# Weight splits, the norm's sum and the order of seven products moved in a two-layer RG-LRU and attention trunk

## The chip, the cores and the metric

The kernel runs on one core of a Trainium2 chip. The metric is the time of one execution on the device in microseconds, as the median of several runs. Three runs of the kernel before took 1909.01, 1909.31 and 1905.85 us, with a median of 1909.01. The profile is of one further execution.

## The reference

The model has two layers on 512 tokens of width 1024, all in float32. Each layer adds half a gated FFN, a mixer, and half a second gated FFN. The mixer is a gated linear recurrence in layer 0 and stick-breaking attention in layer 1; keys and values are projected once, between the layers.

```python
def rms_norm(x, gain):
    xf = x.astype(jnp.float32)
    y = xf * lax.rsqrt(jnp.mean(xf * xf, axis=-1, keepdims=True) + EPS)
    return (y * gain.astype(jnp.float32)).astype(x.dtype)

def swiglu(h, w13, w2):
    gate, up = jnp.split(h @ w13, 2, axis=-1)
    return (jax.nn.silu(gate) * up) @ w2

# per layer: x += 1/2 swiglu(rms_norm(x)); x += mixer(rms_norm(x)); x += 1/2 swiglu(rms_norm(x))
```

The hidden width of an FFN is 2816. The change touches the four FFNs and what prepares them.

## The kernel before

**Layout and precision.** The residual x lies in SBUF as eight tiles of 128 channels by 512 tokens. Each float32 operand is split into a high part in the rounded format that TensorE takes (a cast) and a low part (the operand minus its high part). A product of two operands is three matmuls: high by high, high by low, low by high. A full product of a weight tile of 128 outputs by 1024 inputs with x is so 3 x 8 = 24 matmuls of 128 x 512 (`product`).

**Weights.** The class `Weights` holds a list of all weight tiles in the order of use. SyncE's queue loads a tile into a buffer w_raw, ScalarE casts it to w_hi (L85, in some places GpSimd, L87), and VectorE or GpSimd subtracts to get w_lo (L89); the last argument of `plan_w` names the engine of the low part. Tiles are prepared four ahead of the one in use. There are five buffers each of w_hi and w_lo and seven of w_raw.

**The FFN.** Its 22 tiles of hidden channels are worked off in three groups (8, 8 and 6), each followed by eight down products. The first tiles of an FFN are plain ones (six in ffn1 of layer 0, four in ffn2 of both layers, none in ffn1 of layer 1): a gate product pg and an up product pu take x times the gain without the norm's factor, and `swish` multiplies both by the factor r afterwards. All further tiles come in pairs, whose four blocks of weights by two halves of tokens are computed with seven products of half size in place of eight, 24 matmuls of 128 x 256 each, in the order of the table `FORMS`. An entry names a block of weights (a11, a12, a21, a22 as loaded; s1 to s4 are sums that VectorE forms at L114), one of three PSUM banks X, Y, Z that it is added to, and which of the seven forms of the operands it takes. After some of the products a copy on ScalarE or an add or subtraction on VectorE takes what the bank holds (L386 to L397). There are 37 such pairs: 8, 9, 11 and 9.

**Operands of the pairs.** `normed` makes them for two of the eight tiles of x at a time, so it is called four times per FFN: x times gain times r on VectorE, four sums, and the casts and low parts of seven forms (hh and hl). It needs r.

**The norm.** `Norm.add` squares a tile of x on ScalarE and adds it on VectorE to acc; `rstd` sums acc over the channels with one matmul, ss, and turns it into r (three activations on ScalarE, three operations on VectorE, the last gives rs). In the first FFN the squares come with the splits of x at the start, in `split_x`; there pg and pu of tile 0 are issued interleaved, and rstd stands after tile 1. In the two ffn2 the products pg and pu of tile 0 are interleaved by `product2` (seven eighths of both, then the rest), and rstd follows them. Behind rstd, `normed` is called twice and then `swish` of the oldest plain tile, until no tile waits.

**Order.** A scheduler orders the instructions of all engines; at the start the orders of VectorE, SyncE and ScalarE are those of the code (`manual_schedule`). Each engine works its list in order. PSUM has eight banks, given out in turn to the products.

Of the kernel before, what the change touches and what calls it, by code (L numbers as in the profile page):

```python
# [7 lines left out]
F32 = mybir.dt.float32  # L8
# [4 lines left out]
P = 128  # L13
S = 512
D = 1024
KT = D // P
# [6 lines left out]
BLOCKS = ("a11", "a21", "a22", "a12")  # L23
SUMS = {"s3": ("a11", "a21"), "s1": ("a21", "a22"), "s2": ("s1", "a11"), "s4": ("s2", "a12"), **{b: None for b in BLOCKS}}

FORMS = (("a11", "X", 4), ("s3", "Y", 0), ("s2", "X", 1), ("a12", "Z", 5), ("s1", "X", 2), ("a22", "Y", 3), ("s4", "X", 6))
HS = S // 2
NH = 16
HD = 64
# [120 lines left out]
def trunk(ctx, tc, a, out):  # L150
# [60 lines left out]
    def plan_w(key, src, hi="act", lo="dve", cols=1024):  # L211
        plan.append((key, src, cols, hi, lo))

    def plan_ffn(n, l):
        nf = PLAIN[n, l]
        for lo, hi in THIRDS:
            for i in range(lo, hi):
                if i < nf:

                    for j, g in enumerate("gu"):  # L220
                        plan_w((n, l, g, i), a[f"{n}_w13"][l, j, i], lo="pool" if i > 0 else "dve")
                elif i % 2 == 0:
                    for f in FORMS:
                        plan_w((n, l, i, f[0]), a[f"{n}_s13"][l, i // 2])
            for m in range(KT):
                plan_w((n, l, "d", lo, m), a[f"{n}_w2"][l, m, :, lo * P:hi * P], cols=(hi - lo) * P)
# [22 lines left out]
    W = Weights(nc, plan, wp)  # L249
# [102 lines left out]
    def ffn(n, l, ht, g, rs, after, full=False, hn=None):  # L352
# [2 lines left out]
        hn = [] if hn is None else hn  # L355

        def swish(i, pg, pu, act):
            e = cur.ep.tile([P, 4, S], F32, tag="e", name=f"e{n}{l}{i}")
            tg, tu = e[:, 0], e[:, 1]
            nc.vector.tensor_tensor(out=tg, in0=pg, in1=r, op=ALU.mult)  # L360
            last_silu.append(nc.scalar.activation(out=tg, in_=tg, func=AF.Silu))
            nc.vector.tensor_tensor(out=tu, in0=pu, in1=r, op=ALU.mult)
            nc.vector.tensor_tensor(out=tu, in0=tu, in1=tg, op=ALU.mult)
            act.append(split(tu, "a", f"a{n}{l}{i}"))

        def pair(i, act):
# [3 lines left out]
            for f, (name, bank, form) in enumerate(FORMS):  # L370
                hi, lo = W.get((n, l, i, name))
                new = bank not in banks
                if new:
                    banks[bank] = psum(f"p{bank}{n}{l}{i}")
                ps = banks[bank]
                for c in range(2):
                    o = ps[:, c * HS:(c + 1) * HS]
                    for j in range(KT // 2):
                        ws = slice(c * S + j * P, c * S + j * P + P)
                        xh, xl = hn[j][0][:, form], hn[j][1][:, form]  # L380

                        mm(o, hi[:, ws], xh, new and c == 0 and j == 0, False)
                        mm(o, hi[:, ws], xl, False, False)
                        mm(o, lo[:, ws], xh, False, j == KT // 2 - 1)

                if f == 0:  # L386
                    nc.scalar.copy(out=e[:, 0], in_=ps)  # L387
                elif f == 1:
                    nc.scalar.copy(out=e[:, 2], in_=ps)
                elif f == 2:  # L390
                    nc.scalar.copy(out=e[:, 1], in_=ps)
                elif f == 3:
                    nc.vector.tensor_tensor(out=e[:, 0], in0=ps, in1=e[:, 0], op=ALU.add)
                elif f == 4:
                    nc.vector.tensor_tensor(out=e[:, 2], in0=ps, in1=e[:, 2], op=ALU.subtract)
                elif f == 5:
                    nc.vector.tensor_tensor(out=e[:, 1], in0=ps, in1=e[:, 1], op=ALU.subtract)  # L397
# [13 lines left out]
        for lo_t, hi_t in THIRDS:  # L411
            act = []
            for i in range(lo_t, hi_t):
# [3 lines left out]
                    continue  # L417
                pg, pu = psum(f"pg{n}{l}{i}"), psum(f"pu{n}{l}{i}")
                wg = W.get((n, l, "g", i))
                if i == lo_t:  # L420
                    product2(pg, wg, pu, W.get((n, l, "u", i)), ht, full and lo_t == 0)
                else:
                    product(pg, wg, ht)
                    product(pu, W.get((n, l, "u", i)), ht)
                queue.append((i, pg, pu, act))
                if r is None:
                    if full and i == 0:
                        continue
                    r = rs()
                while queue:  # L430
                    for _ in range(2):
                        if len(hn) < KT // 2:
                            hn.append(normed(len(hn), g, r, f"{n}{l}"))
                    swish(*queue.pop(0))
# [30 lines left out]
    def split_x(k0, k1):  # L465
        for m in range(k0, k1):
            h.append(split_gain(x[m], gain(G_FFN1[0], m), "a", f"h0_{m}"))
            n0.add(m, x[m], [])

    phase_ffn()  # L470
    with tc.manual_schedule(engines={mybir.EngineType.DVE, mybir.EngineType.SP, mybir.EngineType.Activation}):
        W.first(2, ((0, 1), (1, 2), (2, 4), (4, 6), (6, 8)), load_x, split_x)
    late = {}

    def start():
# [224 lines left out]
    for p in range(NPAIR):  # L700
# [19 lines left out]
        run(gen)  # L720
        run(pend)
        pend = gen
        if p in (3, 5, 7):
            h3.append(normed(len(h3), G_FFN1[1], r3, "n3"))

    def v_out(g, pv):
        vt = dp.tile([2, 4, P, NCH, P], F32, tag="vd", name=f"vd{g}", bufs=2)
# [9 lines left out]
    for g in range(2):  # L737
# [5 lines left out]
        for c in range(4):  # L743
# [8 lines left out]
                    mm(pv[s], xl[:, ss], hi[:, ks], False, c == 3 and k == 1)  # L752
            if g == 0 and c < 2:
                run(pend)
            if g == 0 and c == 2:
                h3.append(normed(len(h3), G_FFN1[1], r3, "n3"))
            if g == 1 and c == 0:
                v_out(0, pvs[0])
# [305 lines left out]
```

## Time and profile before

| what | value |
|---|---|
| median of three runs | 1909.01 us |
| profiled execution | 1906.09 us |
| its span, first to last instruction | 1904.4 us |
| TensorE busy | 1846.8 us, 97% |
| VectorE busy | 1392.7 us, 73% |
| ScalarE busy | 921.5 us, 48% |
| GpSimd busy | 216.3 us, 11% |
| HBM traffic | 108 GB/s over the span |

The profile is read from the whole to the part: the busy shares say which engine could set the end, the table of stretches says where that engine was not busy, the list of its waits says for what, and a timeline shows what the engine that it waited for was doing. A group of rows gives a mean over all places where a line runs, so a single wait is found in the timeline alone.

### The profile page before, as it was taken

What the parts mean: (1) busy time and instruction counts of PE and PEld (TensorE: products, weight loads), DVE (VectorE), ACT (ScalarE), POOL (GpSimd) and SP (SyncE); (2) the same over time, 40 slices, a digit from 0 to 9 for tenths busy, and PEclk for the clock granted to TensorE, in tenths of its full rate; (3) what the DMA queues carried; (4) which work ended last, traced back from release to release, by engine and by line L of the source; (5) the groups of instructions that cost most, each with busy time, mean ns of one, the idle gap of its engine ahead of it and who ended that gap; (6) DMA issues with size and microseconds to landing.
All of it is one profiled execution on the core that took longest, in us unless ns stands there. A gap on an engine that the chain in (4) does not pass through costs nothing. (4 is left out here: it accounts for less than half of the span.)

```text
span 1904.4 us, 27318 instructions
## 1 busy us (share of the span) xinstructions
PE 1846.8 (97%) x11040; PEld 1635.3 (86%) x11040; DVE 1392.7 (73%) x1687; ACT 921.5 (48%) x1282; POOL 216.3 (11%) x218
## 2 busy tenths in 40 slices
PE   8899999999999999999899999999888999999999
PEld 6789989887788899897689999898676788999897
DVE  6876757688869577476978658575899869667573
ACT  4434525476645245255545435244578745445251
POOL 5100000021220000000200000000366530000000
PEclk9999999999999999999999999999999999999999
DMA  6132513222423234132363424234365431424131
GB/s 222 56 90 88 150 57 115 67 79 89 144 78 103 86 102 142 45 111 77 122 218 115 133 78 125 86 96 141 125 190 144 146 103 54 133 78 145 66 106 61
DMA packets 73118, 207.87 MB, mean 109 GB/s; under 512 B 7584, under 2 KB 17056, under 8 KB 72480
## 3 DMA queue, kind: packets, MB, share of 16 engines
q1 hardware_dynamic: 72704, 205.81, 35.4%
q8 instruction: 86, 1.41, 0.3%
q10 hardware_dynamic: 288, 0.32, 0.1%
q14 instruction: 40, 0.33, 0.1%
HBM read 189.85 MB, written 16.25 MB: 108 GB/s over the span
## 5 line engine op out<-in xcount | busy, mean ns | idle before, releaser
L85 ACT CAST w_hi<-w_raw 128x1024 fp32r<-128x1024 f32 (+1 forms) x165 | 165.5, 1007 | 287.0 <-PE pdffn L201 82.5
L85 ACT CAST w_hi<-w_s 128x1024 fp32r<-128x1024 f32 x148 | 155.3, 1049 | 238.1 <-PE pdffn L201 104.7
L201 PE MATMUL pXffn<-hhffn,w_hi 128*128 128x256 f32 x832 | 236.7, 285 | 4.7 <-ACT hhffn L342 2.0
L201 PE MATMUL pXffn<-hlffn,w_hi 128*128 128x256 f32 x832 | 236.3, 284 | 0.9 <-DVE hlffn L343 0.8
L201 PE MATMUL pXffn<-hhffn,w_lo 128*128 128x256 f32 x832 | 235.9, 284 | 0.0
L89 DVE TENSOR_TENSOR w_lo<-w_raw,w_hi 128x1024 fp32r<-128x1024 f32 (+3 forms) x169 | 193.1, 1145 | 54.6 <-ACT w_hi L85 49.1
L201 PE MATMUL pdffn<-ahffn,w_hi 128*128 128x512 f32 x592 | 230.8, 390 | 0.3
L201 PE MATMUL pdffn<-alffn,w_hi 128*128 128x512 f32 x592 | 230.7, 390 | 0.0
L201 PE MATMUL pdffn<-ahffn,w_lo 128*128 128x512 f32 x592 | 230.4, 389 | 0.0
L89 DVE TENSOR_TENSOR w_lo<-w_s,w_hi 128x1024 fp32r<-128x1024 f32 x148 | 180.9, 1222 | 45.1 <-ACT w_hi L85 44.8
L85 ACT CAST w_hi<-w_a 128x1024 fp32r<-128x1024 f32 x111 | 116.5, 1049 | 171.0 <-PE pdffn L201 70.7
L201 PEld LDWEIGHTS pXffn<-hhffn,w_hi 128*128 128x128 f32 x832 | 160.1, 192 | 6.5 <-ACT effn L387 2.3
L89 DVE TENSOR_TENSOR w_lo<-w_a,w_hi 128x1024 fp32r<-128x1024 f32 x111 | 135.6, 1222 | 35.8 <-ACT w_hi L85 35.8
L201 PEld LDWEIGHTS pXffn<-hlffn,w_hi 128*128 128x128 f32 x832 | 160.3, 193 | 1.7 <-DVE hlffn L343 1.3
L201 PEld LDWEIGHTS pXffn<-hhffn,w_lo 128*128 128x128 f32 x832 | 160.3, 193 | 0.0
L440 DVE SCALAR_TENSOR_TENSOR x<-pdffn,x 128x512 f32<-128x512 f32 x72 | 49.8, 691 | 137.1 <-PE pdffn L201 137.1
L201 PEld LDWEIGHTS pdffn<-ahffn,w_hi 128*128 128x128 f32 x592 | 111.2, 188 | 24.6 <-ACT ahffn L407 1.8
L201 PEld LDWEIGHTS pdffn<-alffn,w_hi 128*128 128x128 f32 x592 | 111.2, 188 | 24.3 <-DVE alffn L408 1.0
L201 PEld LDWEIGHTS pdffn<-ahffn,w_lo 128*128 128x128 f32 x592 | 111.1, 188 | 22.6
L201 PE MATMUL pYffn<-hlffn,w_hi 128*128 128x256 f32 x416 | 117.9, 283 | 0.2 <-DVE hlffn L347 0.2
L201 PE MATMUL pYffn<-hhffn,w_hi 128*128 128x256 f32 x416 | 117.8, 283 | 0.0
L201 PE MATMUL pYffn<-hhffn,w_lo 128*128 128x256 f32 x416 | 117.7, 283 | 0.0
(1150 smaller groups left out, 4786.5 us busy)
## 6 DMA issues: line engine op xcount, KB each, us to landing
w_a<-in_ffn_s SPq DMA_DIRECT2D x148, 512.0 KB, 3.7
w_raw<-in_ffn_w SPq DMA_DIRECT2D x90, 512.0 KB, 3.8
w_raw<-in_ffn_w SPq DMA_DIRECT2D x32, 384.0 KB, 3.2
w_raw<-in_w_in SPq DMA_DIRECT2D x16, 512.0 KB, 3.6
qp<-qd SPq DMA_DIRECT2D x14, 512.0 KB, 5.3
w_raw<-in_w_out SPq DMA_DIRECT2D x8, 512.0 KB, 3.7
w_raw<-in_w_k SPq DMA_DIRECT2D x8, 512.0 KB, 3.6
w_raw<-in_w_v SPq DMA_DIRECT2D x8, 512.0 KB, 3.7
```

Of the source, the lines that this page charges most:

```text
L85: nc.scalar.copy(out=hi[:, cs], in_=raw[:, cs])
L89: eng.tensor_tensor(out=lo[:, cs], in0=raw[:, cs], in1=hi[:, cs].bitcast(F32), op=ALU.subtract)
L201: nc.tensor.matmul(o, l, r, start=start, stop=stop, skip_group_check=True)
L440: nc.vector.scalar_tensor_tensor(out=x[m], in0=pd, scalar=0.5, in1=x[m], op0=ALU.mult, op1=ALU.add)
```

## The change

The six edits are: the low parts of the plain tiles' weights are made on VectorE, where GpSimd made those of all plain tiles but the first of each FFN; the squares and adds of the first norm come after all splits of the start; in the first FFN `swish` comes ahead of two `normed`, and tiles 0 and 1 of every FFN take other buffers for it; in the two ffn2, pg of tile 0 is a product by itself, rstd follows it, then pu; the operands of the second layer's first FFN are made among the products of the values instead of those of the keys; and the seven products have another order.

```diff
--- before.py
+++ after.py
@@ -23,7 +23,7 @@
 BLOCKS = ("a11", "a21", "a22", "a12")
 SUMS = {"s3": ("a11", "a21"), "s1": ("a21", "a22"), "s2": ("s1", "a11"), "s4": ("s2", "a12"), **{b: None for b in BLOCKS}}
 
-FORMS = (("a11", "X", 4), ("s3", "Y", 0), ("s2", "X", 1), ("a12", "Z", 5), ("s1", "X", 2), ("a22", "Y", 3), ("s4", "X", 6))
+FORMS = (("a11", "X", 4), ("a12", "Z", 5), ("s2", "X", 1), ("s3", "Y", 0), ("s1", "X", 2), ("a22", "Y", 3), ("s4", "X", 6))
 HS = S // 2
 NH = 16
 HD = 64
@@ -216,9 +216,8 @@
         for lo, hi in THIRDS:
             for i in range(lo, hi):
                 if i < nf:
-
                     for j, g in enumerate("gu"):
-                        plan_w((n, l, g, i), a[f"{n}_w13"][l, j, i], lo="pool" if i > 0 else "dve")
+                        plan_w((n, l, g, i), a[f"{n}_w13"][l, j, i])
                 elif i % 2 == 0:
                     for f in FORMS:
                         plan_w((n, l, i, f[0]), a[f"{n}_s13"][l, i // 2])
@@ -355,8 +354,11 @@
         hn = [] if hn is None else hn
 
         def swish(i, pg, pu, act):
-            e = cur.ep.tile([P, 4, S], F32, tag="e", name=f"e{n}{l}{i}")
-            tg, tu = e[:, 0], e[:, 1]
+            if i < 2:
+                tg, tu = temp("sq", f"tg{n}{l}{i}"), temp("acc", f"tu{n}{l}{i}")
+            else:
+                e = cur.ep.tile([P, 4, S], F32, tag="e", name=f"e{n}{l}{i}")
+                tg, tu = e[:, 0], e[:, 1]
             nc.vector.tensor_tensor(out=tg, in0=pg, in1=r, op=ALU.mult)
             last_silu.append(nc.scalar.activation(out=tg, in_=tg, func=AF.Silu))
             nc.vector.tensor_tensor(out=tu, in0=pu, in1=r, op=ALU.mult)
@@ -385,11 +387,11 @@
 
                 if f == 0:
                     nc.scalar.copy(out=e[:, 0], in_=ps)
-                elif f == 1:
+                elif f == 3:
                     nc.scalar.copy(out=e[:, 2], in_=ps)
                 elif f == 2:
                     nc.scalar.copy(out=e[:, 1], in_=ps)
-                elif f == 3:
+                elif f == 1:
                     nc.vector.tensor_tensor(out=e[:, 0], in0=ps, in1=e[:, 0], op=ALU.add)
                 elif f == 4:
                     nc.vector.tensor_tensor(out=e[:, 2], in0=ps, in1=e[:, 2], op=ALU.subtract)
@@ -417,7 +419,12 @@
                     continue
                 pg, pu = psum(f"pg{n}{l}{i}"), psum(f"pu{n}{l}{i}")
                 wg = W.get((n, l, "g", i))
-                if i == lo_t:
+                if i == 0 and not full:
+
+                    product(pg, wg, ht)
+                    r = rs()
+                    product(pu, W.get((n, l, "u", i)), ht)
+                elif i == lo_t:
                     product2(pg, wg, pu, W.get((n, l, "u", i)), ht, full and lo_t == 0)
                 else:
                     product(pg, wg, ht)
@@ -427,6 +434,12 @@
                     if full and i == 0:
                         continue
                     r = rs()
+                if full:
+                    while queue:
+                        swish(*queue.pop(0))
+                        for _ in range(2):
+                            if len(hn) < KT // 2:
+                                hn.append(normed(len(hn), g, r, f"{n}{l}"))
                 while queue:
                     for _ in range(2):
                         if len(hn) < KT // 2:
@@ -465,11 +478,12 @@
     def split_x(k0, k1):
         for m in range(k0, k1):
             h.append(split_gain(x[m], gain(G_FFN1[0], m), "a", f"h0_{m}"))
-            n0.add(m, x[m], [])
 
     phase_ffn()
     with tc.manual_schedule(engines={mybir.EngineType.DVE, mybir.EngineType.SP, mybir.EngineType.Activation}):
         W.first(2, ((0, 1), (1, 2), (2, 4), (4, 6), (6, 8)), load_x, split_x)
+        for m in range(KT):
+            n0.add(m, x[m], [])
     late = {}
 
     def start():
@@ -720,8 +734,6 @@
         run(gen)
         run(pend)
         pend = gen
-        if p in (3, 5, 7):
-            h3.append(normed(len(h3), G_FFN1[1], r3, "n3"))
 
     def v_out(g, pv):
         vt = dp.tile([2, 4, P, NCH, P], F32, tag="vd", name=f"vd{g}", bufs=2)
@@ -752,7 +764,7 @@
                     mm(pv[s], xl[:, ss], hi[:, ks], False, c == 3 and k == 1)
             if g == 0 and c < 2:
                 run(pend)
-            if g == 0 and c == 2:
+            if g == 0 and c > 0 or g == 1 and c == 1:
                 h3.append(normed(len(h3), G_FFN1[1], r3, "n3"))
             if g == 1 and c == 0:
                 v_out(0, pvs[0])
```

**VectorE at the start.** h0_5l to h0_7l are the low parts of the last tiles of x, acc_n0 is the running sum of squares (sq_n00 to sq_n07), w_lo0 and w_lo1 the low parts of tile 0's two weights, w_lo2 and up those of the tiles after it. Before:

```order
L318 SCALAR_TENSOR_TENSOR h0_5l_180<-x1_79,prm_75,h0_5h_179 128x512
L292 TENSOR_TENSOR acc_n0_137<-acc_n0_137,sq_n05_183 128x512
L89 TENSOR_TENSOR w_lo0_107<-w_raw0_105,w_hi0_106 128x256
L89 TENSOR_TENSOR w_lo1_110<-w_raw1_108,w_hi1_109 128x256
L318 SCALAR_TENSOR_TENSOR h0_6l_191<-x1_79,prm_75,h0_6h_190 128x512
L292 TENSOR_TENSOR acc_n0_137<-acc_n0_137,sq_n06_194 128x512
L318 SCALAR_TENSOR_TENSOR h0_7l_198<-x1_79,prm_75,h0_7h_197 128x512
L292 TENSOR_TENSOR acc_n0_137<-acc_n0_137,sq_n07_201 128x512
L486 TENSOR_SCALAR ident_952<-cf_948 128x128
```

And now:

```order
L317 SCALAR_TENSOR_TENSOR h0_5l_164<-x1_79,prm_75,h0_5h_163 128x512
L89 TENSOR_TENSOR w_lo0_107<-w_raw0_105,w_hi0_106 128x256
L89 TENSOR_TENSOR w_lo1_110<-w_raw1_108,w_hi1_109 128x256
L317 SCALAR_TENSOR_TENSOR h0_6l_172<-x1_79,prm_75,h0_6h_171 128x512
L317 SCALAR_TENSOR_TENSOR h0_7l_176<-x1_79,prm_75,h0_7h_175 128x512
L289 COPY acc_n0_181<-sq_n00_179 128x512
L89 TENSOR_TENSOR w_lo2_209<-w_raw2_207,w_hi2_208 128x1024
L291 TENSOR_TENSOR acc_n0_181<-acc_n0_181,sq_n01_183 128x512
L89 TENSOR_TENSOR w_lo3_215<-w_raw3_213,w_hi3_214 128x1024
L291 TENSOR_TENSOR acc_n0_181<-acc_n0_181,sq_n02_186 128x512
L89 TENSOR_TENSOR w_lo4_221<-w_raw4_219,w_hi4_220 128x1024
```

The seven adds that stood between the splits, and the one after them, now stand behind the last split, with a low part of a weight between each two.

**VectorE behind the first norm's factor.** rs_n0 is r; pgffn100 and puffn100 are the products of tile 0, effn100 and effn101 what `normed` works on (before, effn100_382 is the buffer of swish of tile 0). Before, the last of the rows between the factor (row 44 of VectorE) and the end of the first swish:

```order
L343 TENSOR_TENSOR hlffn101_371<-effn101_367,hhffn101_370 128x512
L345 TENSOR_TENSOR effn101_367<-effn101_367 128x256
L347 TENSOR_TENSOR hlffn100_356<-effn100_352,hhffn100_355 128x1024
L345 TENSOR_TENSOR effn101_367<-effn101_367 128x256 x3
L349 SCALAR_TENSOR_TENSOR hlffn101_371<-effn101_367,hhffn101_370 128x256
L360 TENSOR_TENSOR effn100_382<-pgffn100_205,rs_n0_343 128x512
L362 TENSOR_TENSOR effn100_382<-puffn100_206,rs_n0_343 128x512
L347 TENSOR_TENSOR hlffn101_371<-effn101_367,hhffn101_370 128x1024
L114 TENSOR_TENSOR w_s3_13_610<-w_a11_12_574,w_a21_12_576 128x1024
L363 TENSOR_TENSOR effn100_382<-effn100_382 128x512
```

And now, from the factor on:

```order
L308 SCALAR_TENSOR_TENSOR rt_n0_344<-ss_n0_341,rt_n0_344 128x512
L309 SCALAR_TENSOR_TENSOR rs_n0_343<-rt_n0_344,rs_n0_343 128x512
L310 TENSOR_SCALAR rs_n0_343<-rs_n0_343 128x512
L362 TENSOR_TENSOR tgffn100_352<-pgffn100_205,rs_n0_343 128x512
L364 TENSOR_TENSOR tuffn100_353<-puffn100_206,rs_n0_343 128x512
L335 SCALAR_TENSOR_TENSOR effn100_362<-x0_78,prm_75,rs_n0_343 128x512 x2
L344 TENSOR_TENSOR effn100_362<-effn100_362 128x256
L365 TENSOR_TENSOR tuffn100_353<-tuffn100_353,tgffn100_352 128x512
L344 TENSOR_TENSOR effn100_362<-effn100_362 128x256
L335 SCALAR_TENSOR_TENSOR effn101_377<-x0_78,prm_75,rs_n0_343 128x512
L342 TENSOR_TENSOR hlffn100_366<-effn100_362,hhffn100_365 128x512
```

The reads of tile 0's two products now follow the factor at once; before, thirteen rows on operands (45 to 57) stood between. The swish of tile 1 moved with it: it was 38 rows behind the factor and is 19 rows behind it now.

**ScalarE in a pair.** effn216 is the buffer of a pair in the last FFN, pXffn216 and pYffn216 its banks; w_hi369 and up are casts of weights. Before, around the three copies:

```order
L85 CAST w_hi367_15073<-w_s1_365_14999 128x1024
L85 CAST w_hi368_15103<-w_a22_363_14934 128x1024
L387 COPY effn216_15072<-pXffn216_15077 128x512
L407 CAST ahffn214_15064<-effn214_14838 128x512
L407 CAST ahffn215_15068<-effn214_14838 128x512
L85 CAST w_hi369_15135<-w_s4_369_15133 128x1024
L389 COPY effn216_15072<-pYffn216_15107 128x512
L85 CAST w_hi370_15165<-w_raw370_15164 128x1024
L391 COPY effn216_15072<-pXffn216_15077 128x512
```

And now:

```order
L85 CAST w_hi367_15079<-w_s1_365_15003 128x1024
L85 CAST w_hi368_15109<-w_a22_363_14940 128x1024
L409 CAST ahffn214_15070<-effn214_14844 128x512
L409 CAST ahffn215_15074<-effn214_14844 128x512
L389 COPY effn216_15078<-pXffn216_15083 128x512
L85 CAST w_hi369_15141<-w_s4_369_15139 128x1024
L393 COPY effn216_15078<-pXffn216_15083 128x512
L85 CAST w_hi370_15171<-w_raw370_15170 128x1024
L391 COPY effn216_15078<-pYffn216_15176 128x512
L85 CAST w_hi371_15203<-w_raw371_15202 128x1024
```

The copy of the bank Y stood second of three and now stands last, with one cast between it and the copy of X ahead of it.

## Rows read from the trace of the kernel before

**Rows 1.** The page, busy us, share of the span and instructions by engine.

```profile
PE 1846.8 (97%) x11040; PEld 1635.3 (86%) x11040; DVE 1392.7 (73%) x1687; ACT 921.5 (48%) x1282; POOL 216.3 (11%) x218
```

**Rows 2.** Table of stretches: busy us (instructions) by engine, TensorE's clock, DMA share, GB/s.

```profile
0.00:50.00 50.00, 43.70 (x168) 33.76 (x169) 35.29 (x54) 24.33 (x34) 27.14 (x26) 0.93 0.63 211
50.00:100.00 50.00, 43.21 (x216) 36.59 (x214) 43.82 (x61) 23.71 (x32) 6.93 (x2) 0.93 0.20 56
550.00:600.00 50.00, 46.17 (x241) 39.91 (x240) 45.18 (x66) 27.51 (x38) 5.85 (x3) 0.97 0.21 64
1600.00:1650.00 50.00, 47.68 (x349) 45.24 (x350) 41.24 (x48) 25.94 (x35) 0.00 (x0) 1.00 0.48 148
```

**Rows 3.** Waits of TensorE: what waited, for whom, us in total, times, longest.

```profile
PE hsk L201 <- POOL thk L661: 8.2, 6, 2.6
PE pgffn L201 <- DVE effn L360: 5.4, 1, 5.4
PE pXffn L201 <- ACT hhffn L342: 2.0, 1, 2.0
PE pZffn L201 <- DVE w_lo L89: 2.0, 1, 2.0
PE pgffn L201 <- DVE h_7l L318: 1.9, 1, 1.9
PE pXffn L201 <- ACT effn L387: 1.7, 2, 1.5
PE pgffn L201 <- DVE h_6l L318: 1.4, 1, 1.4
PE pXffn L201 <- ACT w_hi L85: 1.0, 1, 1.0
PE pgffn L201 <- DVE h_2l L318: 0.9, 1, 0.9
PE pXffn L201 <- DVE hlffn L343: 0.8, 1, 0.8
PE pgffn L201 <- DVE h_4l L318: 0.8, 1, 0.8
```

**Rows 4.** Table of stretches again: behind three waits, and three others to compare.

```profile
23.50:29.50 6.00, 5.94 (x14) 4.68 (x15) 5.45 (x5) 2.09 (x2) 5.17 (x4) 0.50 0.68 209
30.00:45.00 15.00, 15.00 (x66) 12.02 (x65) 6.05 (x12) 4.80 (x6) 6.62 (x4) 1.00 0.47 140
45.00:75.00 30.00, 26.59 (x118) 21.69 (x116) 30.00 (x42) 13.85 (x19) 9.81 (x3) 0.98 0.06 18
77.00:81.00 4.00, 4.00 (x10) 3.15 (x11) 2.33 (x3) 1.47 (x2) 0.00 (x0) 0.52 0.30 94
586.00:589.40 3.40, 3.40 (x16) 3.40 (x17) 3.40 (x6) 1.79 (x3) 0.00 (x0) 0.50 0.00 0
700.00:720.00 20.00, 20.00 (x169) 20.00 (x169) 17.30 (x19) 10.97 (x14) 0.00 (x0) 1.00 0.43 132
```

**Rows 5.** Timeline of VectorE at the start: start us, duration us, instruction.

```profile
20.05 0.68 DVE L292 TENSOR_TENSOR acc_n<-acc_n,sq_n 128x512 f32<-128x512 f32 x1
20.66 2.85 DVE L318 SCALAR_TENSOR_TENSOR h_7l<-x,prm,h_7h 128x512 fp32r<-128x512 f32 x1
```

**Rows 6.** Timeline of GpSimd, the same place.

```profile
20.48 5.26 POOL L89 TENSOR_TENSOR w_lo<-w_raw,w_hi 128x1024 fp32r<-128x1024 f32 x2 [2.23 <-ACT w_hi L85]
```

**Rows 7.** Timeline of TensorE, the first norm's sum.

```profile
37.89 1.02 PE L298 MATMUL ss_n<-acc_n,onesf 128*128 128x512 f32 x2
```

**Rows 8.** Instructions of L89, by engine: count, duration ns min/median/max, first and last start.

```profile
L89 DVE TENSOR_TENSOR w_lo<-w_raw,w_hi x169: 278/1224/2310, 4.9 to 1880.9; 128x1024 fp32r<-128x1024 f32 x127, 128x768 fp32r<-128x768 f32 x32, 128x256 fp32r<-128x256 f32 x6, 128x128 fp32r<-128x128 f32 x4
L89 POOL TENSOR_TENSOR w_lo<-w_raw,w_hi x23: 2367/2552/3907, 15.8 to 1569.3; 128x1024 fp32r<-128x1024 f32 x23
```

**Rows 9.** Timeline of ScalarE inside a pair of the second FFN.

```profile
701.87 0.58 ACT L391 COPY effn<-pXffn 128x512 f32<-128x512 f32 x1
...
707.35 1.05 ACT L85 CAST w_hi<-w_s 128x1024 fp32r<-128x1024 f32 x1 [2.50 <-DVE w_s L114]
```

## The prediction

> **What bounds the kernel now.** I read the busy shares first, then a table of 50 us stretches, then the list of what TensorE waited for, and last the timelines around the longest of those waits. TensorE is busy for 1846.8 of 1904.4 us [rows 1], so the end is set by its stream of matmuls, and a change that leaves the 11,040 matmuls as they are can only win back pauses between them and matmuls issued at half clock. VectorE stands at 73%, ScalarE at 48%, GpSimd at 11%.
>
> The 50 us table [rows 2] shows where TensorE is not full: 6.3 us missing in the first stretch and 6.8 in the second (both at a granted clock of 0.93), 3.8 in 550 to 600 (0.97), 2.3 in 1600 to 1650. These are the starts of the first FFN, of the second and of the last, the places where plain tiles stand and the four sets of operands for the products by seven are built. In a stretch deep inside an FFN, 700 to 720 [rows 4], TensorE is busy for 20.00 of 20.00.
>
> The list of waits [rows 3] puts names to them. In the first FFN: h_2l 0.9, h_4l 0.8, h_6l 1.4 and h_7l 1.9 (operands split by VectorE too late), then 5.4 in one piece, where a gate product waits for a bank that the swish of tile 1 (L360) has not read yet, then 1.5 for a copy (L387). In the second: hhffn 2.0, hlffn 0.8 and a cast 1.0 (operands of the first pair). In the last: one low part of a weight, 2.0. The largest entry, hsk on GpSimd's thk (8.2), lies in the key stage.
>
> Two of the long pauses and one pair of them are followed by matmuls at half clock [rows 4]: in 23.5 to 29.5 the row has 14 matmuls at 0.50 (6.00/14 = 0.43 us each, against 15.00/66 = 0.227 us in 30 to 45), in 77 to 81 ten at 0.52, in 586 to 589.4 sixteen at 0.50 (0.21 against 20.00/169 = 0.118 us). Before each the engine had stood still: for h_7l, for L360, for hhffn and hlffn.
>
> **The change part by part.**
>
> *Order of the start.* The eight squares of the norm and their adds leave the spaces between the splits, and GpSimd's low parts are gone from there. Now the h_7l split took 2.85 us, with one add of 0.68 just ahead of it (start to start 0.61) [rows 5], while GpSimd had begun two low parts at 20.48 that ran 5.26 us [rows 6]. With seven adds (4.3 us) and this blocking gone, h_6l and h_7l are ready some 4 us earlier, about 16 to 17 us (an estimate; there the loads of x and of the weights are the next limit), before TensorE gets there. So the waits h_6l 1.4 and h_7l 1.9 go, and with them the half clock: 14 x (0.43 - 0.227) = 2.8 us. Sum -6.1. Of h_2l and h_4l (1.7 together) I take nothing, since they follow the loads; the bound is -1.7. What is late next is the sum of squares: behind h_7l stand eight adds and six low parts, 8 x 0.61 + 6 x 1.22 = 12.2 us [rows 5, 8], from about 17.0, so 29.2. TensorE then has first to finish the two first products at about 18.9 and does two more of 24 x 0.227 = 5.45 us each, so it wants the sum at 29.8. Before, it came to it at 37.89 [rows 7]. The slack is 0.6 us; if it is missed, it costs what it is missed by, 0 to 2 us.
>
> *Swish before the operands in the first FFN.* Tile 0 now has its banks read right behind rs_n, tile 1 behind two normed operands instead of four, some 16 us before the gate product of tile 5 wants that bank. The wait of 5.4 goes, and the half clock behind it: 10 x (0.40 - 0.227) = 1.7 us. The L387 copy (1.5) waited for an SBUF buffer that a late swish held; tiles 0 and 1 no longer use those buffers, and it goes. Sum -8.6. Next late is the low part of the up weight of tile 4: VectorE reaches it behind all four operands, about 27.7 us after the sum, and TensorE wants it at 28.4 us (five products of 5.45 us, two matmuls and the sum itself). The slack is 0.7 us; the bound is 2 us lost.
>
> *Low parts on VectorE.* 22 of them, in three FFNs (10, 6 and 6): 22 x 1.22 = 26.8 us more work on VectorE, against 22 x 2.55 us less on GpSimd [rows 8]. Most of it lies where VectorE waits anyway for rs_n. In 45 to 75 it lies on an engine that is busy for 30.00 of 30.00 [rows 4]; there GpSimd ran three low parts for 9.81 us. If each blocks VectorE for its whole length, the move frees 9.81 - 3 x 1.22 = 6.2 us; if none does, it costs 3.7 us. The h_7l row is nearer to the first, so I take this edit as no cost to TensorE, its gain being already counted in the waits above.
> The Trainium skill (Perfetto Trace Analysis, section Optimizing Scalar/DVE Operations) says that where VectorE is saturated, work may be better off on ScalarE or even GpSimd, though GpSimd shares a read port of the SBUF with it and may not help. By the first half the three low parts cost the 3.7 us; by the second they free something. The row on h_7l agrees with the second half; the first is my first rival.
>
> *The sum behind the first gate product.* In the FFNs ffn2 of both layers the norm's sum is issued after 24 matmuls instead of 48, so 24 x 0.227 = 5.4 us earlier, and swish and operands follow. In layer 0 this is more than the waits hhffn 2.0, hlffn 0.8 and the cast 1.0, and the half clock behind (16 x (0.21 - 0.118) = 1.5): -5.3. In layer 1 it frees VectorE early enough for the low part that cost 2.0: -2.0, to -3.5 with the smaller gaps around it. What it adds is that the last operand is wanted 21 matmuls (4.8 us) after the mixer's last product instead of 42; VectorE has it some 3.6 us after by my estimate (an update, a low part of 1.22 that is new there, an add, a split), so 0 to 1 us each may come back.
>
> *Operands of the second layer among the values.* The order of the instructions is the same in the key stage on VectorE, ScalarE and TensorE; only two loads move by a row. The 8.2 us of hsk stay. I take 0, bounds -2 and +2.
>
> *Order of the seven.* Nothing is added or removed. The second product now needs a12 (a block as loaded) rather than s3 (a sum on VectorE), and the copy of the Y bank stands right ahead of its next use. One product is 24 x 0.118 = 2.9 us; the copy takes 0.58 [rows 9] and must be done within the one product s1 between s3 and a22. The row nearest to a trouble is a cast that waited 2.50 us for a sum on VectorE [rows 9]. I take 0 in all 37 pairs; the bound is in the second rival.
>
> **Sum.** -6.1 - 8.6 - 5.3 - 2.0 = -22.0, and with the 1.5 us of smaller gaps in layer 1 it is -23.5. The profiled execution took 1906.1 us (span 1904.4); it becomes 1882.6. It lies 0.15% under the median 1909.0, so as a median that is 1885.5; I say 1885. The terms' own bounds: all of h_2l, h_4l and -2 in the key stage give -27.5, so about 1879 to 1881; both slacks missed and 1 us back at each ffn2 give -17, so 1891.
>
> **Rivals.**
> *VectorE becomes the bound at the starts.* For it: 30.00 of 30.00 in 45 to 75, and slacks of 0.6 and 0.7 us. Against it: the blocking that ends. If low parts come late, a pause of a few us stands again in each of three starts, with the half clock behind it, and about half the gain is left: 1896.
> *A wait in every pair.* Slower. The copy of Y stands behind a cast on ScalarE, and that cast waits for a sum on VectorE: 2.50 + 1.05 + 0.58 = 4.1 us against 2.9 us of s1, so 1.25 us a pair, x 37 = 46; net +23, 1932. It decides from 23.5/37 = 0.64 us a pair. For it: the copy had three products' time before, and has one now. Against it: in the order of after, casts ahead of that copy are at most one, and most are of blocks or of loaded weights that wait for no sum, and ScalarE is busy for 10.97 of 20.00 us there [rows 4].
> *The clock does not come back.* The pauses shrink, but one of 1 to 2 us is left at the first and the second start, and the matmuls behind it still run at half clock; the 6 us of half clock stay and some 3 of waits: 1895.
> *An edit does not do what it says.* The order shows that five of the six do. Only the one among the values is empty; with the two loads that move it is worth 0, within 2 us, which the sum holds already: 1885 still.
>
> **How the numbers follow.** Forecast 0.70 (own range 1879 to 1891), VectorE as bound 0.12, clock 0.06, wait in every pair 0.09, a wash (unforeseen pauses that take all) 0.03. 0.2%, 3.8 us, is about what a measurement of this kernel can tell from no change. Faster: 0.70 + 0.12 + 0.06, less a little for the tails, 0.87; same 0.04; slower 0.09. The range goes from 1878 to 1900.
>
> **What would show it.** Right: no low parts on GpSimd save that of one query weight; h_7l under 1 us and before 18 us; the first sum's matmul near 30 us; no wait of a gate product on the swish; a granted clock of 1.00 from 50 to 100 and 550 to 600; the first pair of the first FFN near 74 us; hsk still near 8 us. Wrong: a wait of pX, pY or pZ on ScalarE's copies or on VectorE's low parts that comes dozens of times (second rival), or single waits on w_lo in the starts (first rival).

## The result and the profile after

The changed kernel takes 1880.36 us as the median of four runs (1879.02 to 1881.04), against 1908.89 for the kernel before in the same comparison. The ratio is 0.9853, with a 95% interval of 0.9836 to 0.987, so 1.3 to 1.6% faster. The forecast was 1885 in a range of 1878 to 1900. The profiled execution took 1879.02 us with a span of 1877.3, 27.1 us less than the span before.

The page's row of busy time shows the same 11,040 matmuls in less time [rows 1], and GpSimd's work down from 216.3 us:

```profile
PE 1839.0 (98%) x11040; PEld 1633.1 (87%) x11040; DVE 1382.4 (74%) x1709; ACT 921.7 (49%) x1282; POOL 156.6 (8%) x196
```

VectorE runs 22 rows more and is yet 10.3 us less busy: 26.8 us of low parts came to it, so its other rows took some 37 us less. The experiments below show what that time was: waiting that the profile counts as busy.

Table of stretches of the kernel after, for the places of [rows 2] (the last FFN now begins 23 us earlier):

```profile
0.00:50.00 50.00, 47.64 (x203) 39.03 (x204) 40.96 (x79) 31.20 (x41) 6.61 (x18) 1.00 0.59 212
50.00:100.00 50.00, 50.00 (x301) 44.64 (x300) 45.88 (x65) 26.41 (x38) 0.00 (x0) 1.00 0.36 125
550.00:600.00 50.00, 49.74 (x362) 47.20 (x361) 45.36 (x58) 27.25 (x37) 0.00 (x0) 1.00 0.33 116
1580.00:1630.00 50.00, 50.00 (x350) 46.87 (x349) 36.66 (x40) 23.19 (x29) 0.00 (x0) 1.00 0.47 159
```

TensorE is full in three of the four or within 0.3 us of it, and the clock is 1.00 in all of them, where the first three had 0.93, 0.93 and 0.97. What stays in the first 50 us is its very start.

The list of TensorE's waits, against [rows 3]:

```profile
PE hsk L201 <- POOL thk L675: 7.4, 5, 2.6
PE z L201 <- DVE spl L862: 5.1, 9, 1.0
PE ri L201 <- ACT xc4h L326: 3.9, 1, 3.9
...
PE pgffn L201 <- DVE h_2l L317: 0.9, 1, 0.9
...
PE pXffn L201 <- ACT effn L389: 0.3, 1, 0.3
```

The waits for h_4l, h_6l, h_7l, L360, hhffn, hlffn, the cast and the last FFN's w_lo are gone; hsk and the waits of the two mixers stay.

Two timelines of the start, VectorE and then TensorE (start us, duration us, instruction), against [rows 5, 7]:

```profile
15.20 0.74 DVE L317 SCALAR_TENSOR_TENSOR h_6l<-x,prm,h_6h 128x512 fp32r<-128x512 f32 x1
15.86 0.74 DVE L317 SCALAR_TENSOR_TENSOR h_7l<-x,prm,h_7h 128x512 fp32r<-128x512 f32 x1
...
28.01 0.69 DVE L291 TENSOR_TENSOR acc_n<-acc_n,sq_n 128x512 f32<-128x512 f32 x1
```

```profile
30.02 0.59 PE L297 MATMUL ss_n<-acc_n,onesf 128*128 128x512 f32 x1
...
74.44 0.28 PE L201 MATMUL pXffn<-hhffn,w_hi 128*128 128x256 f32 x1
```

h_7l takes 0.74 us where it took 2.85, the last add ends at 28.7, 1.3 us before TensorE comes to the sum at 30.0 (37.9 before), and the first pair starts at 74.4.

The clearest view of where the time came from is a table of stages. A stage runs here from its first matmul in TensorE's timeline to the first of the next one; the first counts from the span's start. All in us:

| kernel | first FFN | recurrent mixer | second FFN | keys, values | third FFN | attention | last FFN | span |
|---|---|---|---|---|---|---|---|---|
| before | 373.3 | 163.8 | 352.6 | 105.2 | 342.0 | 213.9 | 353.5 | 1904.4 |
| after | 356.1 | 163.0 | 346.6 | 105.2 | 342.0 | 214.6 | 349.8 | 1877.3 |
| difference | -17.2 | -0.8 | -6.0 | 0 | 0 | +0.7 | -3.7 | -27.1 |

The three FFNs with plain tiles gave 26.9 of the 27.1 us. The third FFN, which has pairs only, is the same to 0.1 us.

### The profile page after: what moved, and what is told of

Read it like the earlier page. It is cut to its first block, busy times and chain, and to the rows that moved or that the text cites. A ratio compares the mean times of both kernels' runs of the same rounds, so it can differ in the third digit from the quotient of the medians.

```text
span 1877.3 us, 27297 instructions
## 1 busy us (share of the span) xinstructions
PE 1839.0 (98%) x11040; PEld 1633.1 (87%) x11040; DVE 1382.4 (74%) x1709; ACT 921.7 (49%) x1282; POOL 156.6 (8%) x196
## 4 chain that ended last, share of the span: by engine, by line
PE 44%; DVE 5%; issue 3%; POOL 2%; ACT 1%; SPq 0%; DMA 0%; POOLq 0%; DVEq 0%; ACTq 0%
PE pdffn L201 13%; PE pXffn L201 12%; PE pYffn L201 6%; PE pZffn L201 3%; PE v L201 2%; PE wo L201 2%; PE k L201 2%; PE puffn L201 1%; PE pgffn L201 1%; DVE spl L862 1%; PE z L201 1%; DVE t L862 1%; DVE sp L852 1%; POOL sph L859 0%; DVE w_lo L89 0%
## 5 line engine op out<-in xcount | busy, mean ns | idle before, releaser
L85 ACT CAST w_hi<-w_s 128x1024 fp32r<-128x1024 f32 x148 | 155.2, 1050 | 254.0 <-PE pdffn L201 105.4
L89 DVE TENSOR_TENSOR w_lo<-w_raw,w_hi 128x1024 fp32r<-128x1024 f32 (+3 forms) x191 | 219.9, 1154 | 76.8 <-ACT w_hi L85 68.2
L89 DVE TENSOR_TENSOR w_lo<-w_s,w_hi 128x1024 fp32r<-128x1024 f32 x148 | 180.8, 1221 | 33.1 <-ACT w_hi L85 33.0
L89 DVE TENSOR_TENSOR w_lo<-w_a,w_hi 128x1024 fp32r<-128x1024 f32 x111 | 135.5, 1222 | 36.2 <-ACT w_hi L85 34.8
```

The lines of the kernel that those rows point to most:

```text
L85: nc.scalar.copy(out=hi[:, cs], in_=raw[:, cs])
L89: eng.tensor_tensor(out=lo[:, cs], in0=raw[:, cs], in1=hi[:, cs].bitcast(F32), op=ALU.subtract)
```

## The experiments

Each kernel below but the last was executed with a profile once, so it is read by its stages. The stages that an edit doesn't touch show what an execution varies by: 0.1 us in the third FFN and in the last, 0.4 in the second, but some 2 us in the first (355.5 in u_sum, 357.9 in i_rec), in the keys and values (104.3 to 106.4) and in the two mixers, whose half-clock stretches come and go. Labels with u_ undo one edit of the changed kernel, those with d_ do one edit alone on the kernel before.

| kernel | first FFN | recurrent mixer | second FFN | keys, values | third FFN | attention | last FFN | span |
|---|---|---|---|---|---|---|---|---|
| u_lo | 369.3 | 163.4 | 351.4 | 104.4 | 342.0 | 215.4 | 353.7 | 1899.5 |
| u_add | 357.3 | 163.8 | 346.7 | 105.4 | 342.0 | 214.5 | 349.8 | 1879.5 |
| u_swish | 363.7 | 164.3 | 347.3 | 105.4 | 342.0 | 215.1 | 349.9 | 1887.7 |
| u_sum | 355.5 | 165.0 | 349.5 | 104.3 | 342.0 | 214.6 | 350.4 | 1881.3 |
| u_forms | 356.0 | 163.0 | 346.1 | 105.4 | 342.0 | 214.6 | 349.8 | 1876.9 |
| u_h3 | 356.3 | 165.2 | 347.0 | 104.3 | 342.1 | 214.9 | 349.8 | 1879.6 |
| d_lo | 358.3 | 164.8 | 349.1 | 104.4 | 342.0 | 214.7 | 351.1 | 1884.5 |
| d_forms | 374.0 | 163.9 | 353.2 | 105.1 | 342.0 | 213.7 | 355.2 | 1907.1 |
| x_twin | 375.8 | 163.6 | 355.6 | 104.3 | 342.0 | 215.2 | 360.3 | 1916.8 |
| i_rec | 357.9 | 158.1 | 346.8 | 105.4 | 342.0 | 214.9 | 349.8 | 1874.8 |
| i_k | 355.9 | 165.1 | 346.6 | 104.8 | 342.0 | 211.0 | 349.8 | 1875.3 |
| i_both | 356.6 | 158.1 | 346.9 | 106.4 | 342.1 | 211.6 | 349.8 | 1871.5 |

**u_lo: the low parts back on GpSimd.**

```diff
-                        plan_w((n, l, g, i), a[f"{n}_w13"][l, j, i])
+                        plan_w((n, l, g, i), a[f"{n}_w13"][l, j, i], lo="pool" if i > 0 else "dve")
```

> The changed kernel with the low parts of the plain tiles back on GpSimd; all else as changed. Theory (GpSimd's low parts hold up VectorE): 22 low parts of about 2.5 us again delay the splits, the sum and the operands; the stage up to the first mixer product is 3 to 8 us longer than the 356.1 us of the changed kernel, the ffn2 of layer 0 (346.6) and of layer 1 (349.8) 1 to 4 us each, and single VectorE rows of 2 us and more beside GpSimd's stand in the starts. Rival (VectorE's load is what counts): 26.8 us less work on VectorE, so all three stages are as long or up to 3 us shorter.

It lost 13.2, 4.8 and 3.9 us in the three FFNs, 21.9 of the 27.1; the rival would have had them the same or shorter. GpSimd's and VectorE's timelines of the start, and TensorE's longest wait in the first 110 us:

```profile
16.15 2.75 POOL L89 TENSOR_TENSOR w_lo<-w_raw,w_hi 128x1024 fp32r<-128x1024 f32 x1 [1.93 <-ACT w_hi L85]
...
27.46 10.33 POOL L89 TENSOR_TENSOR w_lo<-w_raw,w_hi 128x1024 fp32r<-128x1024 f32 x4 [0.60 <-ACT w_hi L85]
```

```profile
15.41 0.74 DVE L317 SCALAR_TENSOR_TENSOR h_7l<-x,prm,h_7h 128x512 fp32r<-128x512 f32 x1
...
16.59 2.85 DVE L291 TENSOR_TENSOR acc_n<-acc_n,sq_n 128x512 f32<-128x512 f32 x1
...
29.99 5.59 DVE L291 TENSOR_TENSOR acc_n<-acc_n,sq_n 128x512 f32<-128x512 f32 x2
```

```profile
PE ss_n L297 <- DVE acc_n L291: 6.0, 1, 6.0
```

The splits now stand ahead of GpSimd's first low part and escape it (h_7l 0.74). The adds of 0.68 do not: 2.85, and 5.59 for two of them beside four low parts in a row. So the sum came 6.0 us late, with half clock from 31.7 to 38.5. The place moved, the cause is the one of [rows 5, 6]. TensorE waited for a low part of GpSimd's itself for 0.2 us in all, so it is not their own lateness that costs. The kernel before, executed on the same chip, had a span of 1902.0: without this edit the other five together gave 2.5 us.

**u_add: the squares and adds back between the splits.**

```diff
             h.append(split_gain(x[m], gain(G_FFN1[0], m), "a", f"h0_{m}"))
+            n0.add(m, x[m], [])
...
-        for m in range(KT):
-            n0.add(m, x[m], [])
```

> The changed kernel with the squares and adds of the first norm back between the splits; low parts stay on VectorE. Theory (the adds themselves make the splits late): seven adds of 0.61 us put h_7l some 4 us later, TensorE waits for h_6l and h_7l 1.5 to 3 us in all, perhaps with half clock behind; first stage 2 to 6 us longer than 356.1. Rival (only GpSimd's blocking made them late): no wait for h_6l or h_7l over 0.5 us and a first stage within 1 us of 356.1. Other stages unchanged in both.

The first FFN is 1.2 us longer, between the two theories and nearer to the rival; the stage varies by more than that, so no cost of this edit is shown. h_7l starts at 18.80, 2.9 us later than in the changed kernel, and TensorE still does not wait for it: it waits 0.6 us for h_4l, and its scheduled order had a product of tile 1 to do meanwhile. TensorE's timeline shows something that the prediction did not have:

```profile
21.21 0.59 PE L297 MATMUL ss_n<-acc_n,onesf 128*128 128x512 f32 x1
```

The sum stands at 21.2 here and at 30.0 in the changed kernel. With GpSimd's low parts gone, the adds behind the splits make the norm's factor later, not earlier: it is ready at 35.0 against 27.9 here.

**u_swish: the swish of tiles 0 and 1 back behind the operands.**

```diff
-            if i < 2:
-                tg, tu = temp("sq", f"tg{n}{l}{i}"), temp("acc", f"tu{n}{l}{i}")
...
-                if full:
-                    while queue:
-                        swish(*queue.pop(0))
...
```

> The changed kernel with the swish of tiles 0 and 1 back behind the operands and in the old buffers. Theory (their place sets when the bank comes free): a gate product waits again for the swish of tile 1, 2 to 6 us, with half clock behind it; first stage 4 to 9 us longer than 356.1. Rival (with VectorE no longer held up the swish comes in time at either place): no such wait, first stage within 1 us.

The first FFN is 7.6 us longer, as the theory had it. The two longest of TensorE's waits of the first 110 us, and the VectorE row that ended the longer one:

```profile
PE pgffn L201 <- DVE effn L359: 3.1, 1, 3.1
PE pXffn L201 <- ACT effn L386: 1.5, 1, 1.5
```

```profile
65.59 0.68 DVE L359 TENSOR_TENSOR effn<-pgffn,rs_n 128x512 f32<-128x512 f32 x1
```

Two of the waits of [rows 3] are back, 3.1 and 1.5 us, the first with half clock from 65.3 to 72.2.

**u_sum: the two first products of ffn2 interleaved again, the sum behind both.**

```diff
-                if i == 0 and not full:
-                    product(pg, wg, ht)
-                    r = rs()
-                    product(pu, W.get((n, l, "u", i)), ht)
-                elif i == lo_t:
+                if i == lo_t:
```

> The changed kernel with pg and pu of tile 0 interleaved again in the two ffn2 and the sum behind both. Theory (the sum's place gives the operands their time): the ffn2 of layer 0 is 3 to 6 us longer than 346.6, with waits for hhffn and hlffn, that of layer 1 1 to 3.5 us longer than 349.8. Rival (the operands were late only because GpSimd held up VectorE): both within 1 us.

The second FFN is 2.9 us longer, the last 0.6. In the second, TensorE's waits are no longer for hhffn and hlffn but for a cast (1.3) and a low part (1.2). Both theories hold a part: of the 6.0 us of the second FFN about half hangs on the sum's place, of the 3.7 of the last 0.6.

**u_forms and u_h3: the old order of the seven; the operands asked for among the keys again.**

```diff
-FORMS = (("a11", "X", 4), ("a12", "Z", 5), ("s2", "X", 1), ("s3", "Y", 0), ...
+FORMS = (("a11", "X", 4), ("s3", "Y", 0), ("s2", "X", 1), ("a12", "Z", 5), ...
```

```diff
+        if p in (3, 5, 7):
+            h3.append(normed(len(h3), G_FFN1[1], r3, "n3"))
...
-            if g == 0 and c > 0 or g == 1 and c == 1:
+            if g == 0 and c == 2:
```

> The changed kernel with the old order of the seven. Theory (worth nothing in the body of an FFN): the ffn1 of layer 1, which has pairs only, stays within 0.5 us of 342.0; at the starts of the other three the second product needs again the third-form sums and their late low parts, so 0 to 3 us in each of the three stages. Rival (the new order costs something in each of the 37 pairs, hidden by larger gains): the ffn1 of layer 1 gets 3 us or more shorter.

> The changed kernel with the operands of the second layer's first FFN asked for among the keys again. Theory (the scheduler puts the same instructions in the same order either way): every stage within 0.5 us of the changed kernel, but for the attention, which differs from run to run by its clock. Rival (the two loads that move matter): the key and value stage is 1 us or more longer than 105.2.

Neither changes anything beyond the spread: with the old order of the seven the three FFNs differ by -0.1, -0.5 and 0.0 us, and the third FFN stays at 342.0 over its 11 pairs. In u_h3 the keys and values are 0.9 us shorter, not longer; u_lo, u_sum and d_lo, which leave that stage alone, have the same 104.3 to 104.4, so it is the spread of the clock.

**d_lo and d_forms: one edit alone on the kernel before.** The edits are those of the diff.

> The kernel before with only the low parts moved to VectorE. Theory (blocking is the main cause, the other edits share the rest): first stage 373.3 us before, now 361 to 368; ffn2 of layer 0 352.7 before, now 349 to 352; of layer 1 353.5 before, now 350 to 353. Rival (VectorE's load is the bound at the starts): 26.8 us more on it, each stage as long as before or longer.

> The kernel before with only the new order of the seven. Theory: no change in the ffn1 of layer 1 (342.1 before, within 0.5), and 0 to 3 us less in the first stage and in each ffn2, whose first pairs waited for operands. Rival (a wait in each pair): 0.3 us a pair or more, 3 us or more longer in the ffn1 of layer 1 with its 11 pairs.

The low parts alone give -15.0, -3.5 and -2.4 us, 20.9 in the three FFNs and 19.9 of the span, more in the first than I expected; the rival, VectorE's load, is refuted. The waits for h_6l, h_7l, L360 and hhffn go with this edit alone. The four longest waits that are left in the first and second FFN:

```profile
PE pZffn L201 <- DVE w_lo L89: 2.0, 1, 2.0
PE pXffn L201 <- ACT effn L387: 1.5, 1, 1.5
...
PE pgffn L201 <- DVE h_2l L318: 0.9, 1, 0.9
...
PE pgffn L201 <- DVE h_4l L318: 0.6, 1, 0.6
```

The waits for L387 (1.5), h_2l and h_4l are those of [rows 3]. The low part's 2.0 is a new one, in the second FFN; the one of [rows 3], in the last, is 1.1 here.

The new order of the seven alone is 0.7, 0.6 and 1.7 us slower in the three FFNs with plain tiles and the same in the third: no wait in the pairs, and no gain at their starts. The first two of these are no more than an execution varies by. Its span of 1907.1 lies among those of other executions of the kernel before (1902.0 to 1909.6), so no loss is shown either.

**x_twin: the same work on GpSimd, for nobody.** GpSimd makes the 22 subtractions a second time, into a scratch buffer that nothing reads.

```diff
         eng.tensor_tensor(out=lo[:, cs], in0=raw[:, cs], in1=hi[:, cs].bitcast(F32), op=ALU.subtract)
+        if twin:
+            nc.gpsimd.tensor_tensor(out=self.scratch, in0=raw[:, cs], in1=hi[:, cs].bitcast(F32), op=ALU.subtract)
```

> The changed kernel, and beside each of the 22 moved low parts GpSimd makes the same subtraction a second time into a scratch buffer that nothing reads. VectorE, ScalarE and TensorE have the same rows in the same order in the first stage. Theory (GpSimd's instruction itself holds up VectorE, whoever needs its result): single VectorE adds and splits take 2 us and more again beside GpSimd's rows, the first norm's sum comes 3 us or more later, and the first stage is 5 to 15 us longer than 356.1. Rival (the kernel before lost time because the low parts came late from a slow engine): nothing waits for GpSimd, VectorE's rows keep their length, the first stage is within 1 us.

The three FFNs lose 19.7, 9.0 and 10.5 us: work whose result nobody wants costs more than the whole change brought. The rival is refuted, but the first stage did not go as I had written: it lost 19.7 us and not 5 to 15, and there something did wait for GpSimd. GpSimd's timeline and its rows of this line (count, duration in ns min/median/max), then VectorE's timeline:

```profile
16.05 21.29 POOL L91 TENSOR_TENSOR scr<-w_raw,w_hi 128x1024 fp32r<-128x1024 f32 x5 [2.10 <-ACT w_hi L85]
37.30 0.29 POOL L502 TENSOR_SCALAR_AFFINE_SELECT cf<-onesf 128x128 f32<-128x128 f32 x1
```

```profile
L91 POOL TENSOR_TENSOR scr<-w_raw,w_hi x22: 2339/2728/11242, 16.1 to 1585.1; 128x1024 fp32r<-128x1024 f32 x22
```

```profile
23.09 1.22 DVE L89 TENSOR_TENSOR w_lo<-w_raw,w_hi 128x1024 fp32r<-128x1024 f32 x1
24.23 0.68 DVE L294 TENSOR_TENSOR acc_n<-acc_n,sq_n 128x512 f32<-128x512 f32 x1
...
37.62 2.35 DVE L503 TENSOR_SCALAR nrest<-cf 128x128 fp32r<-128x128 f32 x1 [9.78 <-POOL cf L502]
```

From 16 to 25 us VectorE worked without a gap at its normal 1.22 and 0.68, and it was GpSimd that stood still: five subtractions took 21.29 us, the first of them 11.2; it ended at 27.3, 2.2 us behind VectorE's first pause. Then VectorE needed a constant (nrest) that GpSimd makes, whose row stood behind those five, and waited 9.78 us; the sum was 12.5 us late. So most of the loss in the first FFN is this wait, and not VectorE's rows held up. In the last FFN no constant is made, and the blocking shows by itself, GpSimd's row and VectorE's:

```profile
1570.67 7.73 POOL L91 TENSOR_TENSOR scr<-w_raw,w_hi 128x1024 fp32r<-128x1024 f32 x3 [1.75 <-issue]
```

```profile
1573.54 5.15 DVE L347 TENSOR_TENSOR effn<-effn 128x256 f32<-128x256 f32 x2
1578.61 0.74 DVE L338 SCALAR_TENSOR_TENSOR effn<-xr,prm,rs_n 128x512 f32<-128x512 f32 x1
```

Two rows that take 0.41 each otherwise took 5.15 beside the last two of GpSimd's three, and the next is normal when they end. Over the whole execution VectorE's 1709 rows took 1414.2 us, where as many took 1382.4 in the changed kernel. The order of the rows in the second and last FFN is not quite that of the changed kernel, so a part of the 9.0 and 10.5 us may be the order's.
The Trainium skill (SBUF — State Buffer, section Who interferes with whom) says that VectorE and GpSimd share a port pair as an exclusive lock: a VectorE instruction with two inputs in SBUF and a GpSimd one that reads SBUF do not run together, and whichever begins second is blocked. The last FFN's timeline agrees: VectorE's two rows, with two inputs, began behind a GpSimd row (1573.54 against 1573.14) and took 5.15 us. The first timeline agrees that the two do not run together, 11.2 us for a GpSimd row, but not on who came second: that row began at 16.05, 0.1 us ahead of VectorE's first low part (16.14), and it was GpSimd's that was held. The row of nrest (2.35 us, 0.22 otherwise) shows that a VectorE row with one input can be held too.

**i_rec, i_k and i_both: the same lesson elsewhere.** GpSimd's casts of the recurrence-branch weights (i_rec), and its casts of the key heads (i_k), go to ScalarE; i_both has both.

```diff
-    plan_w((kind, m), ..., hi="pool" if kind == "rec" else "act")
+    plan_w((kind, m), ..., hi="act")
...
-            nc.gpsimd.tensor_scalar(out=hi, in0=t, scalar1=1.0, scalar2=0.0, op0=ALU.mult, op1=ALU.add)
+            nc.scalar.copy(out=hi, in_=t)
...
-        nc.gpsimd.tensor_scalar(out=hi, in0=y, scalar1=1.0, scalar2=0.0, op0=ALU.mult, op1=ALU.add)
+        nc.scalar.copy(out=hi, in_=y)
```

> The changed kernel with the high parts of the eight recurrence-branch weights cast on ScalarE, where GpSimd casts them. If GpSimd's rows hold up VectorE there too (a 0.69 row took 1.53 beside one), the stage of the recurrent mixer is 1 to 4 us shorter than 163.0 and the wait of 3.9 for xc4h shrinks. Rival (ScalarE's eight casts of 1.05 come at the cost of its own rows there): within 1 us or longer.

> The changed kernel with the two casts of the key heads (thk, khk) on ScalarE, where GpSimd makes them. If the chain from kxk to hsk is what TensorE waits for, it gets some 0.5 us shorter at each head pair (0.62 against 0.7 to 1.1, and no change of engine), the waits for thk shrink from 7.4 to 2 to 5 us and the key and value stage is 2 to 6 us shorter than 105.2. Rival (in ScalarE's order the casts stand behind weights' casts of 1.05): within 1 us or longer.

> The changed kernel with both moves from GpSimd to ScalarE: the casts of the eight recurrence-branch weights and the two casts of the key heads. If the two gains seen one at a time add (4.9 us in the recurrent stage, 0.4 in the key stage and 3.6 in the attention), the profiled span is 1867 to 1871 us and the median 1869 to 1873. If the 3.6 us in the attention were only where the clock fell in that one execution, the median is 1873 to 1877. Rival (the moved casts meet on ScalarE): no better than 1876.

In i_rec the recurrent mixer is 4.9 us shorter (158.1). One VectorE row and GpSimd's beside it in the changed kernel, then the same VectorE row in i_rec, and TensorE's wait there:

```profile
411.54 1.53 DVE L602 SCALAR_TENSOR_TENSOR s<-s,a 128x512 f32<-128x512 f32 x1
```

```profile
411.05 1.48 POOL L87 TENSOR_SCALAR w_hi<-w_raw 128x1024 fp32r<-128x1024 f32 x1
```

```profile
411.65 0.68 DVE L602 SCALAR_TENSOR_TENSOR s<-s,a 128x512 f32<-128x512 f32 x1
```

```profile
PE ri L201 <- ACT xc4h L326: 1.6, 1, 1.6
```

The wait for xc4h fell from 3.9 to 1.6, and the half clock behind it went. ScalarE's cast is also shorter than GpSimd's (1.05 against 1.48), and the two causes were not told apart. i_k missed what it was made for: the key stage is 0.4 us shorter, less than it varies by, and hsk waits 8.8 us, now for ScalarE. It gained 3.6 in the attention, where the two lines also serve the casts of most query heads, which the expectation overlooked: GpSimd has 16 rows less in the key stage and 14 less in the attention. In the attention VectorE's rows took 1.3 us less (182.4 against 183.8) and the granted clock was 1.00 against 0.97; how the moved casts bring the 3.6 us stays open. i_both, timed over five rounds, has a median of 1872.81 us (1872.34 to 1875.2), a ratio to the kernel before of 0.9816 (0.9802 to 0.9829). Its interval lies below that of the changed kernel, so it beats both; the two gains add: 158.1 us again in the recurrent mixer and 211.6 in the attention.

## Why the prediction was right, point by point

**The place and the sign.** The forecast had the gain in the starts of three FFNs, nothing in the pairs and nothing in the key stage, and that is what the stages show.

**The sum.** Forecast -14.7 in the first FFN, -5.3 in the second, -2.0 to -3.5 in the last; measured -17.2, -6.0 and -3.7. It was short by 3.6 us of span in all. The term that was mis-sized is the first. From the start of one matmul to the start of the next, the pause at h_4l, which I had left in place, held 1.0 us and went too; the four pauses that I counted held 1.0 us more than the list of waits gives them, and the half clock behind two of them 0.4 more. The recurrent mixer's -0.8 and the attention's +0.7 are no more than these stages vary by.

**The slacks.** The sum was forecast to be ready at 29.2 for a matmul at 29.8; it was ready at 28.7 for one at 30.0. Neither slack was missed, and the first rival, VectorE as the bound, did not come.

**Which edit pays.** Here the prediction's working was wrong, though its sum was not. It gave the order of the start 6.1 us, the place of the swish 8.6, the sum 5.3 and 2.0, and the low parts nothing of their own. Undone one at a time in the stages they act on, the order of the start costs 1.2, the swish 7.6, the sum 2.9 and 0.6, and the low parts 13.2, 4.8 and 3.9; alone, the low parts give 20.9. The failing step is the sentence on the low parts that takes them "as no cost to TensorE, its gain being already counted in the waits above": in d_lo the waits for h_6l, h_7l, L360 and hhffn go with the low parts alone, and the other edits would each remove part of the same waits. The 6.1 us of the order of the start are not shown at all. The sum came out none the less, because the six edits were made together: a wait that either of two edits removes is gone, whichever it is put down to. The costs of undoing add up to more than the gain (34 us against 27), since one pause can have two edits that would each prevent it.

**The swish is a case of its own.** Behind the operands it costs 7.6 us in the changed kernel. In d_lo, where the old place stands with the old order of the start, no gate product waits for it, and of what stood there before only the copy's wait of 1.5 is left. The traces show the difference: in d_lo the norm's sum stands at 20.3, the factor is ready at 27.0 and L360 of tile 1 begins 32.3 us later, at 59.3; in u_swish the sum stands at 29.6, the factor is ready at 34.6 and L359 begins 31.0 us later, at 65.6. TensorE comes to that bank at 63.8 and 63.3. So what differs is when the sum comes, and u_add shows that the order of the start makes it later (30.0 against 21.2). One of the six edits thus made room for another to be worth 7.6 us; the changed kernel without these two alone was not run.

**The rivals.** A wait in every pair: refuted, 342.0 us in both orders, and no wait of TensorE for the 37 copies of the Y bank. The clock that does not come back: refuted, 1.00 at all three starts. The edit among the values is empty, as forecast.

## What to carry to other kernels

Where a VectorE row takes three times its usual time, look at what GpSimd does in that moment before looking at the row: moving GpSimd's work to the engine that it held up made that engine less busy, not more. Gains read from a list of waits tell how much there is to win, but not which edit wins it; one undo and one edit alone tell that, and only a change of all edits together shows their sum. An engine that nobody waits for is not free when it shares a path with one that is waited for.

## What the runs showed of the hardware

The blocking goes both ways: VectorE working without a gap stretched one GpSimd row of about 2.4 us to 11.2 us (x_twin), while single VectorE rows of 0.41 to 0.75 us took 2.1 to 3.0 beside GpSimd's subtractions (u_lo, x_twin). The profile counts the waiting as busy time on either engine: the 11.2 us of that row, and 31.8 us more for as many rows of VectorE in x_twin. So a share of busy time on the page can be too high for both.
